# An mLSTM input stage without q and k: scores from one product with Wq Wk^T, gate weights folded through the blocks on VectorE

## The chip, the cores and the metric

The kernel runs on one core of one Trainium2 chip. It is written in a tile framework: the program says what is computed in which order, and the framework's scheduler places each engine's instructions and the semaphores between them. The metric is the device time of one execution in microseconds (us); the time before the change is the median of 3 runs, 1916.47 us (1914.49 to 1919.42).

The engines are PE (TensorE, matmuls; its weight loads are listed apart as PEld), DVE (VectorE), ACT (ScalarE), POOL (GpSimd) and SP (SyncE, which here only issues DMA transfers). Each engine works through its own instructions in order and waits on semaphores for the others.

## The reference, cut to what matters

Two layers of a decoder trunk over 256 tokens and 2048 features. The change is in the mLSTM group of layer 0. `xm` is a slice of the input projection, 256 tokens by 2048 channels; it is one of four slices of equal width (the other three belong to an RG-LRU group and to two gate paths). Each of Wq, Wk, Wv is block-diagonal, with 512 blocks of 4 by 4:

```
xmc = silu(causal_dwconv(xm, conv_w, conv_b))
q = block_diag(xmc, Wq);  k = block_diag(xmc, Wk);  v = block_diag(xm, Wv)
qkv = concat(q, k, v)                       # 256 x 6144
ig = qkv @ Wi + bi;  fg = qkv @ Wf + bf     # 8 heads each
# 8 heads of 256 channels, chunkwise; per head:
scores = (q @ k.T) / 16 * exp(decay matrix from ig, fg)
h = (scores @ v + ...) / normaliser
```

After that the kernel normalises each head, gates it, projects the concatenated groups with an output matrix and adds the residual. Layer 1 (RWKV-7) is not touched by the change.

## The kernel before

**The main stream on PE.** The weights of the four projections (input and output of both layers) are loaded in pieces of 256 by 512 (`load_w`, one 512 KB DMA from SP into one of four `raw` buffers). ACT rounds a piece to a high part `whi`, DVE forms the low part `wlo = raw - whi` (`split_w`, line 133 is the wrapper through which all ACT and DVE instructions pass), with three buffers each. `in_proj` goes through the eight pieces of 512 output columns; for a piece, `in_mms` issues 24 matmuls: the weights' high part times the high and the low part of the activations (16), then the low part times the high part (8). These have `gb` (two PSUM banks) as their output.

**The side work.** Everything else (convolutions, gates, recurrences) is written as generators with `yield`s that carry a time; `Weave` calls them between the matmuls of the main stream. PE's order is exactly the order in which the program issues matmuls (`InOrder`), so a side matmul whose operand is late holds up every main matmul behind it. DVE's and ACT's orders come from the scheduler; a piece's `whi` and `wlo` have high priority, and nothing that is emitted later goes ahead of them on their engines (`Behind`). Side results go to one of four `mb` PSUM banks.

**The mLSTM's input, `mlstm_in(c, xm)`.** The 2048 channels are done in four groups `c` of 512 (4 tiles of 128 channels, two heads). The projection of group `c` fills `gb`; ACT copies it to `xm`, and `mlstm_in(c)` runs as side work during the projection of the next group. Its generator's times are longer than that projection, so its last part, all of its matmuls, is issued in one run when `wv_.drain(prev)` empties it at the end of the next `in_proj`. This makes a **cluster** of side matmuls between the last main matmul of a projection and the first of the next. In order:

1. the convolution (ACT, then 3 DVE instructions `xc` a tile), `th` (ACT tanh) and `xm2 = 2 silu` (DVE);
2. `we`: 16 DVE products that spread the 4 by 4 blocks of Wq, Wk, Wv and Wv transposed into 128 by 128 block-diagonal tiles (`qkvs` holds the blocks, `blk` is the mask);
3. 8 matmuls of 256 columns for q and k (`mb<-xm,we` in the profile), copied out with a factor 0.5 by four ACT instructions to `qk`;
4. 8 matmuls of 128 columns for v (`mb<-we,xm`), copied to `vtok` by ACT;
5. 4 matmuls with 40 columns that take the v part of the gates' weights through Wv (`mb<-wif,we`), copied to `gv` by DVE;
6. 12 matmuls with 40 output rows for the gates: q and k against `wiff`, xm against `gv`; they alternate between two halves of the PE array's columns (output rows 0 to 39 and 64 to 103), and DVE adds the two halves to `gacc`;
7. the scores of two heads from `qk` (8 matmuls), copied to `S` by ACT with a factor 1/16.

`wiff` (the gates' weights, 128 by 48 by 40) is one 960 KB DMA in `tables()`, the generator that loads and prepares small tables during the first projection. The tile `wr` of the change takes the memory (tag `wg`) that `wiff` has here.

Of the kernel before, what the change touches and what calls it, by code (L numbers as in the profile page):

```python
# [144 lines left out]
def two_layers(ctx, tc, x, gpost, cst, selc, v0, v1, w_in0, w_out0, w_in1, w_out1, lruw, qkvw,  # L145
               wif, gbias, lora1, lora2, out):
    nc = tc.nc
    act, dve, pool, pe = nc.scalar, nc.vector, nc.gpsimd, nc.tensor
    PS = bass.MemoryType.PSUM
    wv_ = Weave(tc, 4)  # L150
    pe = wv_.pe = InOrder(tc, pe)
    dve, act = Behind(tc, dve), Behind(tc, act)
# [13 lines left out]
    def mbank():  # L166
        return pm.tile([P, 512], F32, name="mb", tag="mb")
# [252 lines left out]
    with ExitStack() as l0:  # L420
# [4 lines left out]
        def t4(name):  # L425
            return tp.tile([P, 4, T], F32, name=name, tag="t4")
# [27 lines left out]
        h = to_features(xs, [scale(ss[tt], s0) for tt in range(2)], lambda i: vs0("pre", i), (0, 0))  # L454


        wiff = c0.tile([P, 2048], F32, name="wif", tag="wg")[:, 0:1920].rearrange("p (a b) -> p a b", a=48)
        qkvs = c0.tile([P, 4, 16, 4], F32, name="qkvs")
# [4 lines left out]

        def tables():
            yield 2.1
            nc.sync.dma_start(qkvs, qkvw)
            nc.sync.dma_start(cs0, cst[:, NC1:NC])
            nc.sync.dma_start(sel, selc)
            nc.sync.dma_start(gbs, gbias)
# [12 lines left out]
            dve.tensor_scalar(s4, lt[:, 0, :], 4.0, None, MUL)  # L482
            dve.tensor_scalar(n4, lt[:, 0, :], -4.0, None, MUL)
            yield 7.7
            nc.sync.dma_start(wiff, wif)
            nc.sync.dma_start(vec1, v1)
            nc.sync.dma_start(cs[:, 128:NC1], cst[:, 128:NC1])
            act.copy(bonesr, cs0[:, 160:288])
# [10 lines left out]
        xm2s = []  # L499

        def mlstm_in(c, xm):
            xc = t4("xc")
            for f in range(4):
                i = 4 * c + f
# [7 lines left out]
            we = [t4("we") for _ in range(2)]  # L512
            wv = [w.rearrange("p a t -> p (a t)").rearrange("p (w f o) -> p w f o", w=2, f=4) for w in we]
            for m in range(4):
                for f in range(4):
                    dve.tensor_tensor(
                        wv[m // 2][:, m % 2, f, :].rearrange("p (b o) -> p b o", o=4),
                        qkvs[:, m, 4 * c + f, :].unsqueeze(1).broadcast_to([P, 32, 4]),
                        blk.unsqueeze(2).broadcast_to([P, 32, 4]), MUL)
                yield 4.0 if m == 3 else 1.0  # L520
            wq, wk, wvv, wvT = (wv[m // 2][:, m % 2] for m in range(4))
            qk = [t4("qk") for _ in range(2)]
# [6 lines left out]
            qt = lambda f: qk[f // 2][:, 2 * (f % 2), :]  # L529
            kt = lambda f: qk[f // 2][:, 2 * (f % 2) + 1, :]  # L530
            for tt in range(2):
                b = mbank()
                for f in range(4):
# [4 lines left out]
            gv = s0.tile([P, 160], F32, name="gv", tag="gv", bufs=1)  # L538
            b = mbank()
            for f in range(4):  # L540
                pe.matmul(b[:, f * 40:(f + 1) * 40], lhsT=wvT[:, f, :], rhs=wiff[:, 32 + 4 * c + f, :],
                          start=(f == 0), stop=True, skip_group_check=True)
            dve.tensor_copy(gv, b[:, 0:160])
            yield 0.96

            ops = []
            for f in range(4):
                i = 4 * c + f
                ops += [(wiff[:, i, :], qt(f)), (wiff[:, 16 + i, :], kt(f)), (gv[:, f * 40:(f + 1) * 40], xm[:, f, :])]
            b = mbank()  # L550
            for n, (w, r) in enumerate(ops):
                o = b[64 * (n % 2):64 * (n % 2) + 40, 0:T]
                pe.matmul(o, lhsT=w, rhs=r, start=(n < 2), stop=(n >= 10), skip_group_check=True)
                if n % 4 == 3:
                    yield 0.5
            for r in (slice(0, 40), slice(64, 104)):
# [5 lines left out]
            for hd in range(2):  # L562
                b = mbank()
                for j, (lo_, w_) in enumerate(((0, T), (P, P))):
                    o = b[:, 0:T] if j == 0 else b[:, T:T + P]
                    for f in range(2):
                        pe.matmul(o, lhsT=kt(2 * hd + f)[:, j * P:(j + 1) * P], rhs=qt(2 * hd + f)[:, lo_:T],
                                  start=(j == 0 and f == 0), stop=(f == 1), skip_group_check=True)
                activ(S[:, 2 * c + hd, :], b[:, 0:384], AF.Copy, scale=0.0625)
                yield 0.8  # L570

        gt = c0.tile([8, 8, T], F32, name="gt", tag="wg")
# [729 lines left out]
```

## Time and profile before

| what | value |
|---|---|
| median of 3 runs | 1916.47 us (1914.49 to 1919.42) |
| the profiled execution, its own time | 1918.1 us |
| its span, first to last instruction | 1916.3 us |
| mean granted TensorE clock | 0.995 |
| HBM read | 289.20 MB |
| the four clusters begin at | 64.35, 99.03, 133.83 and 168.63 us |

The profiled execution is one more run. Its own time is 1.8 us longer than its span, and 1.6 us over the median of the others. A row of a timeline gives the start, the length, the engine, the line, the operation, `out<-in` by the program's names (without buffer numbers), the shapes and the count; a bracket gives idle time ahead of it and what ended it. Lengths of consecutive instructions overlap a little, so the pace of an engine is read from the distance of two starts. A matmul of plain 32-bit floats shows as two records.

### The profile page before, as it was taken

The numbers are of one execution on the slowest core, as the hardware profiler recorded it, in microseconds if no ns is written. First come the engines' busy times: TensorE is split into PE (matmuls) and PEld (weight loads), VectorE is DVE, ScalarE is ACT, GpSimd is POOL, SyncE is SP. The second block draws the span as 40 slices with busy tenths as digits, with TensorE's granted clock in tenths as the row PEclk, the third lists the DMA queues.
The fourth block names the chain that finished last, engine by engine and source line by source line (L and its number), as shares of the span: only waits on it lengthen the run. The fifth ranks groups of instructions, "written<-read, shape, count | busy, mean of one in ns | idle before, by whom it ended". The sixth has DMA issues, their size and how long they took to land.

```text
span 1916.3 us, 39538 instructions
## 1 busy us (share of the span) xinstructions
PE 1890.5 (99%) x16506; PEld 1753.2 (91%) x16507; DVE 1394.7 (73%) x2302; ACT 1045.2 (55%) x1609; POOL 59.1 (3%) x84
## 2 busy tenths in 40 slices
PE   9999999999999999999999999999999999999998
PEld 8999999999888899989999999999999999997886
DVE  5667777767555679879689689597796896895544
ACT  6445666645444546555565555655655655555442
POOL 0000000000000000000000000000000000000000
PEclk9999999999999999999999999999999999999999
DMA  7333544445666444423434334344343433356654
GB/s 254 138 133 111 176 165 171 152 173 197 214 202 202 165 144 147 155 106 137 143 130 143 123 130 157 109 150 146 116 147 133 141 133 133 122 186 201 211 202 156
DMA packets 86947, 299.63 MB, mean 156 GB/s; under 512 B 9576, under 2 KB 12392, under 8 KB 86768
## 3 DMA queue, kind: packets, MB, share of 16 engines
q1 hardware_dynamic: 86768, 297.11, 45.0%
q8 instruction: 129, 2.11, 0.4%
q14 instruction: 50, 0.41, 0.1%
HBM read 289.20 MB, written 7.86 MB: 155 GB/s over the span
## 4 chain that ended last, share of the span: by engine, by line
PE 93%; DVE 4%; ACT 1%; issue 1%; DMA 1%; POOL 0%; SPq 0%; DVEq 0%; POOLq 0%; ACTq 0%
PE gb L117 75%; PE mb L117 17%; DVE wlo L133 2%; PE mb L120 1%; ACT whi L133 1%; DVE wb L133 1%; DMA raw<-in_w_in_dram 0%; DVE rt L133 0%; DVE Tb L133 0%; DMA xq<-in_x_dram 0%; DVE tf L133 0%; DVE Ab L133 0%; DVE yT L133 0%; ACT ZT L133 0%; ACT vt L133 0%
## 5 line engine op out<-in xcount | busy, mean ns | idle before, releaser
L133 DVE TENSOR_TENSOR wlo<-raw,whi 128x1024 fp32r<-128x1024 f32 x509 | 619.6, 1218 | 344.2 <-ACT whi L133 308.4
L133 ACT CAST whi<-raw 128x1024 fp32r<-128x1024 f32 x509 | 532.3, 1048 | 553.4 <-PE gb L117 505.1
L117 PE MATMUL gb<-hh,whi 128*128 128x256 f32 x3120 | 793.5, 290 | 2.9 <-ACT whi L133 2.9
L117 PE MATMUL gb<-hl,whi 128*128 128x256 f32 x3120 | 773.7, 284 | 0.5 <-DVE hl L133 0.5
L117 PEld LDWEIGHTS gb<-hh,whi 128*128 128x128 f32 x3120 | 598.8, 192 | 13.6 <-ACT whi L133 3.7
L117 PEld LDWEIGHTS gb<-hl,whi 128*128 128x128 f32 x3120 | 600.0, 192 | 1.9 <-DVE hl L133 1.1
L117 PE MATMUL gb<-hh,wlo 128*128 128x256 f32 x3120 | 454.0, 286 | 0.0
L117 PEld LDWEIGHTS gb<-hh,wlo 128*128 128x128 f32 x3120 | 405.5, 192 | 4.2 <-issue 0.7
L117 PE MATMUL gb<-whi,yl 128*128 128x512 f32 x500 | 136.9, 392 | 0.5 <-DVE yl L133 0.5
L117 PE MATMUL gb<-whi,yh 128*128 128x512 f32 x500 | 136.5, 392 | 0.0
L117 PE MATMUL gb<-wlo,yh 128*128 128x512 f32 x500 | 135.7, 390 | 0.0
L117 PEld LDWEIGHTS gb<-whi,yl 128*128 128x128 f32 x500 | 93.2, 188 | 20.4 <-DVE yl L133 0.9
L117 PEld LDWEIGHTS gb<-wlo,yh 128*128 128x128 f32 x500 | 93.5, 188 | 19.7
L117 PEld LDWEIGHTS gb<-whi,yh 128*128 128x128 f32 x500 | 93.0, 188 | 19.3
L133 DVE TENSOR_TENSOR Tb<-Tb,tf 64x31 f32<-64x31 f32 (+15 forms) x248 | 82.5, 333 | 6.1
L133 DVE TENSOR_TENSOR tf<-Ab,Tb 64x31 f32<-64x31 f32 (+15 forms) x248 | 81.8, 330 | 4.5
L117 PE MATMUL mb<-AR,BK 64*128 64x128 f32 (+1 forms) x1024 | 58.0, 253 | 7.0 <-DVE AR L133 6.0
L117 PEld LDWEIGHTS mb<-AR,BK 64*128 64x128 f32 (+1 forms) x1024 | 50.2, 161 | 13.3 <-PE gb L117 7.1
L133 DVE TENSOR_TENSOR UV<-mb,Gn 64x256 f32<-64x256 f32 x64 | 26.9, 421 | 34.6 <-PE mb L117 33.4
L133 ACT ACTIVATE zz<-kP,dv 128x256 f32<-128x256 f32 x64 | 32.3, 505 | 22.9 <-DVE kP L133 12.4
L117 PEld LDWEIGHTS mb<-UV,At 128*64 128x64 f32 (+1 forms) x1024 | 35.0, 137 | 10.3 <-issue 2.2
L1140 POOL TENSOR_TENSOR vr<-vr,mhalf 128x8 f32<-128x8 f32 x16 | 28.3, 1771 | 505.5 <-DVE vr L133 505.5
(259 smaller groups left out, 1859.7 us busy)
## 6 DMA issues: line engine op xcount, KB each, us to landing
raw<-in_w_in_dram SPq DMA_DIRECT2D x384, 512.0 KB, 3.2
raw<-in_w_out_dram SPq DMA_DIRECT2D x128, 512.0 KB, 4.2
y1d<-zt SPq DMA_DIRECT2D x7, 512.0 KB, 3.5
yraw<-y1d SPq DMA_DIRECT2D x7, 512.0 KB, 3.8
l<-in_lora_dram SPq DMA_DIRECT2D x8, 384.0 KB, 4.3
xq<-in_x_dram SPq DMA_DIRECT2D x8, 256.0 KB, 4.4
lw<-in_lruw_dram SPq DMA_DIRECT2D x4, 512.0 KB, 4.9
xr<-in_x_dram SPq DMA_DIRECT2D x8, 256.0 KB, 6.3
```

The costliest lines, as they stand in the source:

```text
L117: return self._chain(self.eng.matmul(*a, **k))
L120: return self._chain(self.eng.transpose(**k))
L133: r = op(*a, **k)
L1140: pool.tensor_tensor(vr, vr, mhalf[:, 0:8], ALU.pow)
```

## The change

- q and k are no longer formed. With X = Wq Wk^T (again 4 by 4 blocks), the scores are xmc X xmc^T. `tables()` loads the blocks of Wk four times over (`krep`, four DMAs), so that each partition holds all four rows of its block, and DVE forms the blocks of X in `Xc` by one product and one reduction. The cluster has 4 matmuls for `pp = X^T xm2` in place of the 8 for q and k, and the scores are taken from `pp` and `xm2`, with the factor 1/64.
- The gates' weights are multiplied by Wq, Wk and Wv beforehand, on DVE. Each `mlstm_in(c)` loads its part of them with each row repeated for the four rows of its block (`wr`, 24 DMAs of 40 KB), multiplies by the blocks (6 instructions `wr<-wr,qkvs`), reduces four ways (4 instructions, into `gw` and `gx`) and adds the two halves (2 instructions). The gates are then 8 matmuls, of `gw` against `xm2` and `xm`. The 4 matmuls and the copy for `gv` are gone, and so is the 960 KB DMA.
- Of the 16 products `we` a group, 8 are left (X and Wv).

The diff, cut to its core:

```diff
+        qkvs = c0.tile([P, 3, 16, 4], F32, name="qkvs")
+        krep = c0.tile([P, 4, 16, 4], F32, name="krep")
+        Xc = c0.tile([P, 4, 16], F32, name="Xc")
+        rows = lambda w: w.rearrange("(b o) r -> b o r", o=4)
...
-            nc.sync.dma_start(qkvs, qkvw)
+            nc.sync.dma_start(qkvs, qkvw[:, 0:3])
+            for i in range(4):
+                nc.sync.dma_start(krep[i:P:4].rearrange("p j t o -> p j (t o)"), rows(qkvw[:, 1].rearrange("p t o -> p (t o)")))
...
-            nc.sync.dma_start(wiff, wif)
+
+            dve.tensor_tensor(krep, krep, qkvs[:, 0].unsqueeze(1).broadcast_to([P, 4, 16, 4]), MUL)
+            dve.tensor_reduce(Xc, krep, mybir.AxisListType.X, ADD)
+            dve.tensor_scalar(qkvs[:, 0:2], qkvs[:, 0:2], 0.5, None, MUL)
...
         def mlstm_in(c, xm):
+            wr = c0.tile([P, 2, 3, 2, 160], F32, name="wr", tag="wg")
+            for o2 in range(2):
+                for m in range(3):
+                    src = rows(wif[:, 16 * m + 4 * c:16 * m + 4 * c + 4].rearrange("p t n -> p (t n)"))[:, 2 * o2:2 * o2 + 2]
+                    for i in range(4):
+                        nc.sync.dma_start(wr[i:P:4, o2, m], src)
...
-            for m in range(4):
+            for m in range(2):
...
-                yield 4.0 if m == 3 else 1.0
+                yield 1.0
+            wx, wvv = we[:, 0], we[:, 1]
+
+            gw = s0.tile([P, 2, 160], F32, name="gw", tag="gw", bufs=1)
+            gx = s0.tile([P, 160], F32, name="gx", tag="gx", bufs=1)
+            for o2 in range(2):
+                for m in range(3):
+                    w = qkvs[:, m, 4 * c:4 * c + 4, 2 * o2:2 * o2 + 2].rearrange("p t o -> p o t")
+                    r = wr[:, o2, m].rearrange("p o (t n) -> p o t n", t=4)
+                    dve.tensor_tensor(r, r, w.unsqueeze(3).broadcast_to([P, 2, 4, 40]), MUL)
+                for to, ms in ((0, slice(0, 2)), (1, slice(2, 3))):
+                    d = gx if o2 else gw[:, to]
+                    dve.tensor_reduce(d, wr[:, o2, ms].rearrange("p m o n -> p n (m o)"), mybir.AxisListType.X, ADD)
+                    if o2:
+                        dve.tensor_tensor(gw[:, to], gw[:, to], gx, ADD)
+                    yield 1.5
+            pp = t4("pp")
+            for f2 in range(2):
                 b = mbank()
-                pe.matmul(b[:, 0:T], lhsT=wq[:, f, :], rhs=xm2[:, f, :], start=True, stop=True, skip_group_check=True)
-                pe.matmul(b[:, T:2 * T], lhsT=wk[:, f, :], rhs=xm2[:, f, :], start=False, stop=True, skip_group_check=True)
-                activ(qk[f // 2][:, 2 * (f % 2):2 * (f % 2) + 2, :], b.rearrange("p (a t) -> p a t", a=2), AF.Copy, scale=0.5)
+                for f in range(2):
+                    pe.matmul(b[:, f * T:(f + 1) * T], lhsT=wx[:, 2 * f2 + f, :], rhs=xm2[:, 2 * f2 + f, :],
+                              start=(f == 0), stop=True, skip_group_check=True)
+                act.copy(pp[:, 2 * f2:2 * f2 + 2, :], b.rearrange("p (a t) -> p a t", a=2))
                 yield 0.6
...
-            for f in range(4):
-                pe.matmul(b[:, f * 40:(f + 1) * 40], lhsT=wvT[:, f, :], rhs=wiff[:, 32 + 4 * c + f, :],
-                          start=(f == 0), stop=True, skip_group_check=True)
-            dve.tensor_copy(gv, b[:, 0:160])
-            yield 0.96
...
-                ops += [(wiff[:, i, :], qt(f)), (wiff[:, 16 + i, :], kt(f)), (gv[:, f * 40:(f + 1) * 40], xm[:, f, :])]
+                ops += [(gw[:, 0, f * 40:(f + 1) * 40], xm2[:, f, :]), (gw[:, 1, f * 40:(f + 1) * 40], xm[:, f, :])]
...
-                        pe.matmul(o, lhsT=kt(2 * hd + f)[:, j * P:(j + 1) * P], rhs=qt(2 * hd + f)[:, lo_:T],
+                        pe.matmul(o, lhsT=xm2[:, 2 * hd + f, j * P:(j + 1) * P], rhs=pp[:, 2 * hd + f, lo_:T],
```

On PE nothing else moves: outside the four clusters its order is the same. Two places show what the scheduler makes of the rest.

DVE around the second cluster (group `c = 1`), before. `wlo` is the main stream's low part; the first `wlo` here belongs to the last but one piece that can be prepared ahead of the cluster, the second waits until PE is done with the last piece ahead of the cluster; `xc` is already the convolution of the next group:

```order
L133 TENSOR_TENSOR wlo<-raw,whi 128x1024
L133 TENSOR_TENSOR we<-qkvs,cs_112 128x128 x9
L133 TENSOR_TENSOR wlo<-raw,whi 128x1024
L133 TENSOR_TENSOR we<-qkvs,cs_112 128x128 x3
L133 SCALAR_TENSOR_TENSOR xc<-xm,vec_97,xc 128x255
L133 COPY gv<-mb 128x160
L133 SCALAR_TENSOR_TENSOR xc<-xm,vec_97,xc 128x254
L133 SCALAR_TENSOR_TENSOR xc<-xm,vec_97,xc 128x255
L133 SCALAR_TENSOR_TENSOR xc<-xm,vec_97,xc 128x253
L133 SCALAR_TENSOR_TENSOR xc<-xm,vec_97,xc 128x254
L133 SCALAR_TENSOR_TENSOR xc<-xm,vec_97,xc 128x253
L133 TENSOR_TENSOR gacc<-gacc,mb 40x256 x2
```

The same place after the change, from the `wr` product that follows the last `we` (five `we` stand between the first `wlo` and this row) to the last sum `gw`, which the gates' matmuls need:

```order
L133 TENSOR_TENSOR wr<-wr,qkvs 128x320
L133 TENSOR_REDUCE gw<-wr 128x160
L133 TENSOR_TENSOR wlo<-raw,whi 128x1024
L133 TENSOR_REDUCE gw<-wr 128x160
L133 TENSOR_TENSOR wr<-wr,qkvs 128x320 x3
L133 TENSOR_REDUCE gx<-wr 128x160
L133 SCALAR_TENSOR_TENSOR xc<-xm,vec_97,xc 128x255
L133 TENSOR_TENSOR gw<-gw,gx 128x160
L133 SCALAR_TENSOR_TENSOR xc<-xm,vec_97,xc 128x254
L133 TENSOR_REDUCE gx<-wr 128x160
L133 SCALAR_TENSOR_TENSOR xc<-xm,vec_97,xc 128x253
L133 TENSOR_TENSOR gw<-gw,gx 128x160
```

Two of the six products stand earlier, among the previous `xc`. Four products, all the reductions and both sums stand here, behind `wlo` and between the next group's `xc`. The other three clusters have the same order (in the fourth, `yc` of the RG-LRU's convolution stands where `xc` does).

SP from the first projection to the second group, before (`raw` are the main stream's pieces, the first piece is ahead of these rows):

```order
L218 DMA raw<-in_w_in_dram 128x1024 x4
L485 DMA wif<-in_wif_dram 128x1920
L486 DMA vec_81<-in_v_dram 128x384
L487 DMA cs<-in_cst_dram 128x386
L218 DMA raw<-in_w_in_dram 128x1024 x34
```

and after:

```order
L218 DMA raw<-in_w_in_dram 128x1024 x4
L493 DMA vec_81<-in_v_dram 128x384
L494 DMA cs<-in_cst_dram 128x386
L218 DMA raw<-in_w_in_dram 128x1024 x4
L514 DMA wr<-in_wif_dram 32x2x160 x24
L218 DMA raw<-in_w_in_dram 128x1024 x14
L514 DMA wr<-in_wif_dram 32x2x160 x24
L218 DMA raw<-in_w_in_dram 128x1024 x8
```

Four times 24 small DMAs now stand between the pieces. Each DMA takes one of eight completion semaphores in turn and waits until the DMA that had it before has landed; from the second batch on the first of the 24 also waits until DVE has read the last `wr`.

More of the change, by code (lines that the diff above doesn't have):

```diff
@@ L454, in two_layers @@
         h = to_features(xs, [scale(ss[tt], s0) for tt in range(2)], lambda i: vs0("pre", i), (0, 0))
-        wiff = c0.tile([P, 2048], F32, name="wif", tag="wg")[:, 0:1920].rearrange("p (a b) -> p a b", a=48)
-        qkvs = c0.tile([P, 4, 16, 4], F32, name="qkvs")
+        qkvs = c0.tile([P, 3, 16, 4], F32, name="qkvs")
+        krep = c0.tile([P, 4, 16, 4], F32, name="krep")
+        Xc = c0.tile([P, 4, 16], F32, name="Xc")
+        rows = lambda w: w.rearrange("(b o) r -> b o r", o=4)
         sel = c0.tile([8, 8, P], F32, name="sel")
@@ L511, in mlstm_in @@
             dve.scalar_tensor_tensor(xm2, th, 1.0, xc, ADD, MUL)
-            we = [t4("we") for _ in range(2)]
-            wv = [w.rearrange("p a t -> p (a t)").rearrange("p (w f o) -> p w f o", w=2, f=4) for w in we]
-            for m in range(4):
+            we = t4("we").rearrange("p a t -> p (a t)").rearrange("p (w f o) -> p w f o", w=2, f=4)
+            for m in range(2):
                 for f in range(4):
+                    i = 4 * c + f
                     dve.tensor_tensor(
-                        wv[m // 2][:, m % 2, f, :].rearrange("p (b o) -> p b o", o=4),
-                        qkvs[:, m, 4 * c + f, :].unsqueeze(1).broadcast_to([P, 32, 4]),
+                        we[:, m, f, :].rearrange("p (b o) -> p b o", o=4),
+                        (Xc[:, :, i] if m == 0 else qkvs[:, 2, i, :]).unsqueeze(1).broadcast_to([P, 32, 4]),
@@ L519, in mlstm_in @@
                         blk.unsqueeze(2).broadcast_to([P, 32, 4]), MUL)
-                yield 4.0 if m == 3 else 1.0
-            wq, wk, wvv, wvT = (wv[m // 2][:, m % 2] for m in range(4))
-            qk = [t4("qk") for _ in range(2)]
-            for f in range(4):
+                yield 1.0
[13 more added lines that the diff above has]
+                    yield 1.5
@@ L528, in mlstm_in @@
                 yield 0.6
-            qt = lambda f: qk[f // 2][:, 2 * (f % 2), :]
-            kt = lambda f: qk[f // 2][:, 2 * (f % 2) + 1, :]
             for tt in range(2):
@@ L537, in mlstm_in @@
                 yield 0.78
-            gv = s0.tile([P, 160], F32, name="gv", tag="gv", bufs=1)
-            b = mbank()
-            for f in range(4):
-                pe.matmul(b[:, f * 40:(f + 1) * 40], lhsT=wvT[:, f, :], rhs=wiff[:, 32 + 4 * c + f, :],
-                          start=(f == 0), stop=True, skip_group_check=True)
-            dve.tensor_copy(gv, b[:, 0:160])
-            yield 0.96
             ops = []
             for f in range(4):
-                i = 4 * c + f
-                ops += [(wiff[:, i, :], qt(f)), (wiff[:, 16 + i, :], kt(f)), (gv[:, f * 40:(f + 1) * 40], xm[:, f, :])]
+                ops += [(gw[:, 0, f * 40:(f + 1) * 40], xm2[:, f, :]), (gw[:, 1, f * 40:(f + 1) * 40], xm[:, f, :])]
             b = mbank()
@@ L552, in mlstm_in @@
                 o = b[64 * (n % 2):64 * (n % 2) + 40, 0:T]
-                pe.matmul(o, lhsT=w, rhs=r, start=(n < 2), stop=(n >= 10), skip_group_check=True)
+                pe.matmul(o, lhsT=w, rhs=r, start=(n < 2), stop=(n >= 6), skip_group_check=True)
                 if n % 4 == 3:
@@ L566, in mlstm_in @@
                     for f in range(2):
-                        pe.matmul(o, lhsT=kt(2 * hd + f)[:, j * P:(j + 1) * P], rhs=qt(2 * hd + f)[:, lo_:T],
+                        pe.matmul(o, lhsT=xm2[:, 2 * hd + f, j * P:(j + 1) * P], rhs=pp[:, 2 * hd + f, lo_:T],
                                   start=(j == 0 and f == 0), stop=(f == 1), skip_group_check=True)
-                activ(S[:, 2 * c + hd, :], b[:, 0:384], AF.Copy, scale=0.0625)
+                activ(S[:, 2 * c + hd, :], b[:, 0:384], AF.Copy, scale=0.015625)
                 yield 0.8
```

## Prediction

> **What bounds the kernel now.** I read the page first, then the chain that ended last, then the stretch that the change touches.
>
> ```profile
> span 1916.3 us, 39538 instructions
> PE 1890.5 (99%) x16506; PEld 1753.2 (91%) x16507; DVE 1394.7 (73%) x2302; ACT 1045.2 (55%) x1609; POOL 59.1 (3%) x84
> PE 93%; DVE 4%; ACT 1%; issue 1%; DMA 1%; POOL 0%; SPq 0%; DVEq 0%; POOLq 0%; ACTq 0%
> ```
>
> PE is never without work for long and makes up 93% of the chain. So PE work that goes away shortens the time, as long as PE does not wait in its place. The second cluster, as PE ran it:
>
> ```profile
> 99.03 3.62 PE L117 MATMUL mb<-xm,we 128*128 128x256 f32 x16
> 102.48 1.95 PE L117 MATMUL mb<-we,xm 128*128 128x128 f32 x16
> 104.27 0.98 PE L117 MATMUL mb<-wif,we 128*128 128x40 f32 x8
> 105.18 0.63 PE L117 MATMUL mb<-qk,wif 128*40 128x256 f32 x4
> ...
> 108.07 2.88 PE L117 MATMUL mb<-qk 128*128 128x256 f32 x16
> 110.71 0.36 PE L117 MATMUL gb<-hh,whi 128*128 128x256 f32 x1
> ```
>
> From start to start: 3.45 us for q and k, 1.79 for v, 0.91 for `gv`, 2.89 for the twelve gate matmuls, 2.64 for the scores, 11.68 in all, no bracket with idle time. DVE and ACT meanwhile:
>
> ```profile
> 96.47 1.23 DVE L133 TENSOR_TENSOR wlo<-raw,whi 128x1024 fp32r<-128x1024 f32 x1
> 97.62 1.90 DVE L133 TENSOR_TENSOR we<-qkvs,cs 128x128 f32<-128x128 f32 x9
> 99.44 1.22 DVE L133 TENSOR_TENSOR wlo<-raw,whi 128x1024 fp32r<-128x1024 f32 x1
> 100.57 0.69 DVE L133 TENSOR_TENSOR we<-qkvs,cs 128x128 f32<-128x128 f32 x3
> 104.89 0.48 DVE L133 SCALAR_TENSOR_TENSOR xc<-xm,vec,xc 128x255 f32<-128x255 f32 x1 [3.63 <-ACT xc L133]
> 105.40 0.32 DVE L133 COPY gv<-mb 128x160 f32<-128x160 f32 x1
> 105.64 2.17 DVE L133 SCALAR_TENSOR_TENSOR xc<-xm,vec,xc 128x254 f32<-128x254 f32 x5
> ```
>
> DVE has its `we` ready when PE begins (99.03) and then idles 3.63 us. It sits off the path, with room; but the change puts its new work just here.
>
> **What goes from PE.** Of q and k half, 3.45 / 2 = 1.73 us; all of `gv`, 0.91; of the gates 4 of 12, 2.89 / 3 = 0.96. That is 3.60 us a cluster, 14.4 us in four. The scores and v stay as they are.
>
> **What PE must now wait for.** After the change PE is done with `pp` and v at 99.03 + 1.73 + 1.79 = 102.55 and comes to the gates, the second of which needs the last sum into `gw`. When is it ready? I go through DVE's new order with these rows:
>
> ```profile
> L133 DVE TENSOR_TENSOR we<-qkvs,cs 128x128 f32<-128x128 f32 x64 | 14.2, 285 | 0.0
> L133 DVE TENSOR_TENSOR Dt<-Dt,S 128x384 f32<-128x384 f32 x8 | 4.4, 554 | 2.1 <-ACT Dt L133 2.0
> L133 DVE TENSOR_REDUCE vr<-yT 128x8 f32<-128x512 f32 x8 | 5.5, 687 | 2.6 <-ACT yT L133 2.4
> ```
>
> Products of 128 and 384 elements take 285 and 554 ns: 1.05 ns an element over about 150 ns. A reduction of 512 elements, 687 ns, lies on the same line, so I price reductions by their input. Nine `we` follow each other at (99.44 - 97.62) / 9 = 0.20 us, some 0.08 less than one lasts, so I take 0.08 off each for the overlap: 0.40 us for a `wr` product or a reduction of 320, 0.74 for one of 640, 0.24 for a sum of 160; 0.42 for an `xc` (five in 2.17) and 1.13 for `wlo` (99.44 to 100.57).
>
> - Five `we` and one product from 97.62: 99.03. The first reduction (640): 99.77.
> - `wlo`, free to run since 99.44 as before, now runs from 99.77 to 100.90.
> - Reduction (320) 101.30; three products 102.51; about 0.1 for the wait on the last of them; reduction (640) 103.35.
> - `xc`, sum, `xc`, reduction (320), `xc`: 0.42 + 0.24 + 0.42 + 0.40 + 0.42 = 1.90, to 105.25. ACT has the input of `xc` ready: its two copies of `xm` and its convolution stand behind two copies `pp` where four `qk` stood.
> - The last sum ends 0.32 later, 105.57, and about 0.1 for the semaphore: PE goes on at 105.67.
>
> So PE waits from 102.55 to 105.67, 3.1 us, but for one gate matmul of 0.24 between the two sums. Seven more gates at 0.24: 107.36, where 108.07 was. **Of the 3.60 us a cluster, 0.7 are left: 2.8 us in four.** Queued behind the waiting gate are the scores and the whole next projection, since PE's order is fixed.
>
> **What the wait does to the clock.** In layer 1 the trace has stretches in which PE's clock is at half. Two of them, each behind the 3.41 us ahead of it (a row gives the busy time of PE, PEld, DVE, ACT and POOL, then the granted clock):
>
> ```profile
> 824.25:827.66 3.41, 2.59 (x30) 2.30 (x31) 3.24 (x10) 0.51 (x1) 0.00 (x0) 1.00 0.44 156
> 827.66:831.08 3.42, 3.42 (x19) 3.42 (x18) 1.50 (x4) 1.55 (x3) 0.00 (x0) 0.50 0.00 0
> 1059.77:1063.18 3.41, 3.11 (x73) 2.86 (x72) 3.35 (x7) 3.34 (x7) 0.00 (x0) 1.00 0.65 251
> 1063.18:1066.60 3.42, 3.42 (x19) 3.42 (x18) 0.41 (x1) 1.27 (x2) 0.00 (x0) 0.50 0.47 161
> ```
>
> And PE's instructions at full clock, at half clock, and in the third of these stretches:
>
> ```profile
> 821.86 0.28 PE L117 MATMUL gb<-hh,whi 128*128 128x256 f32 x1
> 821.98 0.28 PE L117 MATMUL gb<-hl,whi 128*128 128x256 f32 x1
> ...
> 828.09 0.41 PE L117 MATMUL gb<-hh,whi 128*128 128x256 f32 x1
> 828.30 0.41 PE L117 MATMUL gb<-hl,whi 128*128 128x256 f32 x1
> ...
> 1060.44 2.21 PE L117 MATMUL mb<-TT,ZT 32*32 32x32 f32 x64 [0.30 <-ACT ZT L133]
> ```
>
> Ahead of a half-clock stretch PE was busy for 2.59 and 3.11 us of 3.41, but 2.21 us of the latter were matmuls on a 32 by 32 corner: what counts is work of the whole array, and 1.2 us of it (3.41 - 2.21) did not hold the clock. A 3.41 us stretch that takes in the 3.1 us wait holds far less; one that catches only part of it still has gates on 40 of 128 columns beside it. I estimate that in 9 of 10 positions the clock falls. The price: main matmuls 0.21 us apart instead of 0.12, so 3.42 x (1 - 0.12 / 0.21) = 1.5 us at most, about 1.2 as part of the slow stretch falls into the wait itself. Four clusters: 4 x 0.9 x 1.2 = 4.3 us. Before, the clock stays full in the clusters:
>
> ```profile
> 99.03:110.80 11.77, 11.77 (x83) 9.52 (x82) 5.93 (x16) 5.98 (x12) 0.00 (x0) 1.00 0.22 82
> ```
>
> The Trainium skill, "TensorE: Matmul & The Clock Gate", section "What's actually happening", says that the clock falls to half after at least one idle window of about 3.4 us. The row 1059.77:1063.18, busy for 3.11 us, contradicts that reading. By it the wait, broken by one gate, would cost no clock; the rival "the clock stays" below is worked out from rows alone.
>
> **DVE's reads.** The reductions read elements 640 bytes apart. The trace has products on 31 elements 128 bytes apart (747.21, first step of the recursion) and on 31 adjacent ones (798.57, last step):
>
> ```profile
> 747.21 0.20 DVE L133 TENSOR_TENSOR Tb<-Tb,tf 64x31 f32<-64x31 f32 x1
> 798.57 0.18 DVE L133 TENSOR_TENSOR Tb<-Tb,tf 64x31 f32<-64x31 f32 x1
> ```
>
> 0.02 us over 31 elements is 0 to 0.65 ns each. The late reductions have 640 + 320 + 640 + 320 = 1920 elements: 0 to 1.2 us a cluster, 0 to 5 us in all. A gain is excluded, as nothing makes a reduction shorter than its pace here. I take 0.1 us a cluster, near the lower end, since the difference may be a constant. The Trainium skill, "SBUF — State Buffer", section "Specifications (TRN2)", says that SBUF has 16-byte lines and that each step to another line costs something; it gives no price, and the two rows allow little of it.
>
> **SP and the start.** SP's rows:
>
> ```profile
> 0.73 1.82 SPq L437 DMA_DIRECT2D xq<-in_x_dram  x4
> 66.00 0.33 SPq L218 DMA_DIRECT2D raw<-in_w_in_dram  x1
> 80.44 0.33 SPq L218 DMA_DIRECT2D raw<-in_w_in_dram  x1
> raw<-in_w_in_dram SPq DMA_DIRECT2D x384, 512.0 KB, 3.2
> ```
>
> Issues follow at 1.82 / 4, some 0.47 us, so 24 take 11 us. From the second batch on they stand in a gap of SP of 14.4 us, between two pieces (66.00 and 80.44). They may start when the previous `wr` is read, at the last reduction (about 70), and end near 82: the next piece comes 2 us late and lands 3.2 later, while PE needs it 24 matmuls of 0.12, 2.9 us, ahead of the cluster at 99.03. Hidden. The first batch stands among the pieces at the end of the first projection and holds the next one up by at most its 11 us, which four buffers of 2.9 us each about cover; with `krep`'s four DMAs ahead of the second piece, and without the 960 KB, I take 0.3 us for both (0 to 2). Fewer ACT copies and fewer `we` are off the path: nothing.
>
> **Sum** against the profiled execution: 1918.1 - 2.8 + 4.3 + 0.4 + 0.3 = 1920.3, so +2.2. The median of the runs is 1.6 lower; on it the change gives 1918.7, and I predict 1919.
>
> **Rivals.**
> - *The clock stays* (or falls in few clusters): -2.8 + 0.7 = -2.1, 1914.4 on the median. For it: the threshold is read from two places. Against: the two pairs of rows above. Chance 0.17.
> - *The sums are ready in time*, and PE keeps the full 14.4: 1902. Against: `wlo` cannot start before 99.44, and with it 5.8 us of DVE work stand ahead of the last sum's end, while PE arrives at 102.55. Chance 0.05.
> - *Slower, by the reductions*: 160 short groups or distant reads at twice the pace add 1.05 x 1920 = 2.0 us a cluster to the wait, 8 us, and another 1 us of clock: 1928. It decides (over 0.3%, 5.7 us) from 0.5 ns an element. For it: no row has short groups. Against: the rows of reductions and of distant elements. Chance 0.2.
> - *Slower, by SP*: with 1 us an issue, first batch and gap overflow; 24 us instead of 11 put the pieces, by my estimate, some 9 us too late once and 2.5 us three times, 1935. Against: no issue lasts over 0.47. Chance 0.05.
>
> **How the numbers follow.** My forecast has 0.53. About 0.3% is what a measurement of this kernel tells from no change. Faster: the second rival and a tail of the first, 0.07. Slower: the third but for its small end, SP, a tail of the forecast, 0.26. Same: 0.67. The range leaves out the full gain, SP and the upper end of the reductions: 1912.5 to 1927.
>
> **What would show it.** PE idle of about 3 us in each cluster, ended by DVE `gw`; the gates starting 6.6 us after the cluster's begin; a half-clock stretch after most clusters; reductions of 0.82 us (640) and 0.49 (320); `raw` landing before ACT wants it. A cluster without that idle time, or waits on `raw`, would make the prediction wrong.

## The result and the profile after

The changed kernel takes 1930.95 us (median of 4 runs, 1927.7 to 1932.02), the kernel before 1916.22 (1914.49 to 1919.42): ratio 1.0072, 95% interval 1.0054 to 1.009. It is slower by some 14 us, where "the same, 1919" was forecast. The profiled execution took 1927.7 us. One execution of the run with sums in place of reductions was in a slower state (2261.03 us, granted clock 0.747) and is not in that run's median.

Page of the changed kernel (span, busy time by engine, shares of the chain), then PE's longest entry in the list of waits (us in total, times, longest):

```profile
span 1925.9 us, 39475 instructions
PE 1883.1 (98%) x16410; PEld 1742.0 (90%) x16411; DVE 1411.4 (73%) x2317; ACT 1040.6 (54%) x1601; POOL 59.0 (3%) x84
PE 89%; DVE 6%; ACT 1%; issue 1%; SPq 1%; DMA 1%; POOL 0%; DVEq 0%; POOLq 0%; ACTq 0%
PE mb L117 <- DVE gw L133: 14.7, 8, 3.3
```

PE works 7.4 us less than before (1890.5 - 1883.1), yet the span is 9.6 longer: DVE has come into the chain, and PE waits for `gw` eight times, twice a cluster. Where the loss has arisen shows the chain, in which the same long piece of the output projection of layer 0 begins at 468.35 before (first row) and at 480.36 after (second):

```profile
468.35 174.61 PE gb L117 x768
```

```profile
480.36 174.59 PE gb L117 x768
```

In these two executions 12.0 us stand by the end of layer 0. (2.4 of it do not show at the end: layer 1 of the changed kernel happened to have 3 half-clock stretches in it and not 5, besides one at the very end of both.) The medians lie further apart, 14.7 us; the profiled execution is the fastest of the four. The second cluster of the changed kernel on PE; brackets are the idle time ahead of a row:

```profile
103.65 1.89 PE L117 MATMUL mb<-xm,we 128*128 128x256 f32 x8
105.38 1.95 PE L117 MATMUL mb<-we,xm 128*128 128x128 f32 x16
110.14 0.60 PE L117 MATMUL mb<-xm,gw 128*40 128x256 f32 x2 [2.82 <-DVE gw L133]
111.47 3.53 PE L117 MATMUL mb<-xm,gw 128*40 128x256 f32 x14 [0.73 <-DVE gw L133]
114.93 2.92 PE L117 MATMUL mb<-pp,xm 128*128 128x256 f32 x16
```

The cluster begins at T = 103.65. PE is through with v at T + 3.52, as forecast, and passes the second gate at 111.47 = T + 7.82, where T + 6.64 was forecast. The gates behind it take 3.46 us in place of some 1.7: the clock. The stretch that holds the wait, and the one behind it (busy PE, PEld, DVE, ACT, POOL, then the granted clock):

```profile
108.20:111.60 3.40, 0.73 (x4) 0.28 (x6) 3.40 (x9) 0.52 (x2) 0.00 (x0) 1.00 0.30 120
111.60:115.00 3.40, 3.40 (x15) 1.30 (x13) 1.17 (x3) 0.00 (x0) 0.00 (x0) 0.50 0.21 57
```

All four clusters have such a half-clock stretch; PE was busy for 0.60 to 1.26 us of the 3.40 ahead of it. DVE ahead of the gates, in the same cluster:

```profile
103.81 0.48 DVE L133 TENSOR_TENSOR wr<-wr,qkvs 128x320 f32<-128x320 f32 x1
104.21 1.27 DVE L133 TENSOR_REDUCE gw<-wr 128x160 f32<-128x640 f32 x1
105.40 1.21 DVE L133 TENSOR_TENSOR wlo<-raw,whi 128x1024 fp32r<-128x1024 f32 x1
106.53 0.48 DVE L133 TENSOR_REDUCE gw<-wr 128x160 f32<-128x320 f32 x1
...
108.14 1.23 DVE L133 TENSOR_REDUCE gx<-wr 128x160 f32<-128x640 f32 x1
```

The products and the reductions of 320 last what was forecast (0.48); the reductions of 640 last 1.25, not 0.82. And the first product starts at T + 0.16 where the forecast had it end at T. SP and the first pass: the first 24 issues, what ACT then waits for, and PE:

```profile
25.75 16.13 SPq L514 DMA_DIRECT2D wr<-in_wif_dram  x24
41.98 1.95 SPq L218 DMA_DIRECT2D raw<-in_w_in_dram  x4
```

```profile
45.50 1.04 ACT L133 CAST whi<-raw 128x1024 fp32r<-128x1024 f32 x1 [2.23 <-DMA raw<-in_w_in_dram]
46.59 0.39 PE L117 MATMUL gb<-hh,whi 128*128 128x256 f32 x1 [1.58 <-ACT whi L133]
```

An issue takes 16.13 / 24 = 0.67 us, not 0.47; the next piece of `raw` is late, and PE waits, which the four buffers were to prevent. How late the first cluster then begins varies: at 66.85 us here (64.35 before), at 66.35 to 71.37 in the traces of the five experiments below that keep the 24 issues on SP. Where PE's wait at this place is 2.6 us or more (three of the six traces) a half-clock stretch follows, where it is 1.6 to 1.9 us (the other three) none does.

### The profile page after: what moved, and what is told of

It is laid out like the page before. It is cut to its first block, busy times and chain, and to the rows that moved or that the text cites. A ratio compares the mean times of both kernels' runs of the same rounds, so it can differ in the third digit from the quotient of the medians.

```text
span 1925.9 us, 39475 instructions
## 1 busy us (share of the span) xinstructions
PE 1883.1 (98%) x16410; PEld 1742.0 (90%) x16411; DVE 1411.4 (73%) x2317; ACT 1040.6 (54%) x1601; POOL 59.0 (3%) x84
## 4 chain that ended last, share of the span: by engine, by line
PE 89%; DVE 6%; ACT 1%; issue 1%; SPq 1%; DMA 1%; POOL 0%; DVEq 0%; POOLq 0%; ACTq 0%
PE gb L117 72%; PE mb L117 15%; DVE wlo L133 2%; PE mb L120 1%; SPq L514 1%; ACT whi L133 1%; DVE wb L133 1%; DMA raw<-in_w_in_dram 1%; DVE wr L133 0%; DVE gx L133 0%; DVE gw L133 0%; DVE rt L133 0%; DVE we L133 0%; DVE Tb L133 0%; DVE hl L133 0%
## 5 line engine op out<-in xcount | busy, mean ns | idle before, releaser
L133 DVE TENSOR_TENSOR wlo<-raw,whi 128x1024 fp32r<-128x1024 f32 x509 | 619.6, 1218 | 340.1 <-ACT whi L133 307.0
L133 ACT CAST whi<-raw 128x1024 fp32r<-128x1024 f32 x509 | 532.3, 1048 | 549.1 <-PE gb L117 492.5
L133 DVE TENSOR_TENSOR Tb<-Tb,tf 64x31 f32<-64x31 f32 (+15 forms) x248 | 82.6, 333 | 6.1
L133 DVE TENSOR_TENSOR tf<-Ab,Tb 64x31 f32<-64x31 f32 (+15 forms) x248 | 81.9, 330 | 4.5
L133 DVE TENSOR_TENSOR UV<-mb,Gn 64x256 f32<-64x256 f32 x64 | 26.9, 421 | 34.2 <-PE mb L117 33.1
L133 ACT ACTIVATE zz<-kP,dv 128x256 f32<-128x256 f32 x64 | 32.3, 505 | 22.9 <-DVE kP L133 12.4
L117 PE MATMUL mb<-UV,At 128*64 128x64 f32 (+1 forms) x1024 | 43.8, 228 | 0.0
```

Source lines behind the costliest of these rows:

```text
L117: return self._chain(self.eng.matmul(*a, **k))
L133: r = op(*a, **k)
```

## The experiments

The theory to begin with: a late start of 2.5 us, and 2.1 to 2.3 us from one cluster to the next, because the wait for `gw` and the half clock behind it eat more than the removed work. Rivals: the small transfers are the main loss; or VectorE as a whole is late. Each ratio below is to the kernel before, run beside the experiment (medians 1915.37 to 1917.10 us), so times of different experiments are best compared by their ratios.

**Gates behind the scores.**

```diff
-            ops = [] ... 8 gate matmuls (16 records), gacc
             for hd in range(2):
                 ... 8 score matmuls (16 records)
+            ops = [] ... 8 gate matmuls (16 records), gacc
```

> The change with one edit: in each cluster the 16 gate matmuls are issued behind the 16 of the scores instead of ahead of them. Theory (the changed kernel loses 12.0 us by the end of layer 0: about 2.5 at the start behind the longer DMA issue, and 4 x 2.3 in the clusters, where PE waits 2.8 + 0.7 us for gw and then runs 3.4 us at half clock): the scores last 2.6 us at full clock and fill most of the wait; what is left is about 0.3 + 0.7 us a cluster. That alone is 4 x 2.5 = 10 us; where the half-clock stretch goes too, 4 x 1.6 more. Time 1914 to 1921, same or slightly faster than before. Rival A (the transfers and their issue are the main loss, the wait only shows it): less than 3 us gained, 1928 or more. Rival B (VectorE as a whole is too late, so that PE then waits for wlo in the next products instead): about half, 1925, with a row of waits for wlo.

Measured: 1928.32 us, ratio 1.0067 (1.0055 to 1.0079). The theory missed by over 7 us. The time is rival A's. VectorE is late, as rival B had it, but PE waits for `xm`, `we` and `gw`, not for `wlo`. Part of the loss lies at the start: in this execution the first cluster began at 69.50 us, 2.65 later than in the changed kernel, behind a longer wait for `raw`. Cluster 1 waited 0.24 + 0.73 us for `gw`, at full clock; the third cluster shows what happens to the others, on PE, then on ACT and DVE:

```profile
141.22 1.53 PE L117 MATMUL mb<-xm,we 128*128 128x256 f32 x6 [1.95 <-DVE xm L133]
...
150.12 0.60 PE L117 MATMUL mb<-xm,gw 128*40 128x256 f32 x2 [1.92 <-DVE gw L133]
```

```profile
134.22 1.05 ACT L133 CAST whi<-raw 128x1024 fp32r<-128x1024 f32 x1 [6.35 <-DMA raw<-in_w_in_dram]
```

```profile
135.31 1.23 DVE L133 TENSOR_TENSOR wlo<-raw,whi 128x1024 fp32r<-128x1024 f32 x1 [6.17 <-ACT whi L133]
```

DVE stands 6.17 us at a `wlo` whose `raw` is late, with the convolution, `xm` and the fold queued behind it. SP says why `raw` is late: 24 issues begin when the last reduction has read the previous `wr`, and `raw` goes on only behind them:

```profile
113.47 16.36 SPq L514 DMA_DIRECT2D wr<-in_wif_dram  x24
129.92 13.20 SPq L218 DMA_DIRECT2D raw<-in_w_in_dram  x7
```

So there is a ring: last sum of `gw`, 16 us of SP, `raw`, `whi`, `wlo`, convolution, `xm`, next `gw` (the run with one DMA and gates last, below, tests it). Its length is near 37 us (the first gates stand at 76.03, 112.79, 150.12, 187.26), and in the changed kernel this bound lies hidden just behind the wait for `gw`.

**One DMA in place of 24.** The host lays `wif` and Wk out with the rows repeated (no arithmetic):

```diff
-            for o2 in range(2): for m in range(3): for i in range(4):
-                        nc.sync.dma_start(wr[i:P:4, o2, m], src)
+            nc.sync.dma_start(wr.rearrange("p a m o r -> p (a m o r)"), wif[:, c, :])
-            for i in range(4):
-                nc.sync.dma_start(krep[i:P:4]..., ...)
+            nc.sync.dma_start(krep, qkvw[:, 4:8])
```

> The change with one edit: wr and krep come from arrays laid out in the order of the tiles (rows repeated four times), so that one DMA a cluster stands in place of 24 and one in place of 4; the bytes that land are the same. Theory: only the start is lost to the issue (first product piece 0.6 us late, the one at 46.6 us 1.6 us late, 2.5 in all); the clusters keep their wait and their half clock. Time 1928 to 1929, the wait for gw stays 14 to 15 us. Rival A (the issue on SP and the transfers are the main loss): 8 us or more gained, 1923 or less. Rival B (the bytes, not the issue, delay raw): no gain, 1930.5 to 1931.5.

Measured: 1927.3 us, 1.0058 (1.0046 to 1.007): 3.6 less than the changed kernel's 1930.95, a little more than the theory. The intervals of the two ratios overlap, but the end of layer 0 also comes 3.8 us earlier in the trace (476.58, not 480.36). The wait for `gw` stays (13.9 us). By itself SP costs the start (the first cluster begins at 64.15, not 66.85) and little else; the third cluster had two half-clock stretches this time and the fourth none.

**Sums in place of reductions.**

```diff
-                    dve.tensor_reduce(d, wr[:, o2, ms].rearrange("p m o n -> p n (m o)"), X, ADD)
+                    if to == 0:
+                        dve.tensor_tensor(wr[:, o2, 0], wr[:, o2, 0], wr[:, o2, 1], ADD)
+                    dve.tensor_tensor(d, wr[:, o2, 2 * to, 0], wr[:, o2, 2 * to, 1], ADD)
```

> The change with one edit: each of the four strided reductions of a cluster is replaced by sums of two contiguous rows (for the pair of 640: one sum of 320 and one of 160; for that of 320: one of 160). Theory (the reductions of 640 at 1.25 us are what made the wait longer than forecast): VectorE's path to the last gw gets shorter by 2 x (1.19 - 0.40 - 0.24) + 2 x (0.40 - 0.24) = 1.4 us a cluster, PE's wait by the same, 5.6 us in all: 1925. If the shorter wait also saves some of the half-clock stretches, 1.6 us for each of them more: down to 1919. Rival (the place in VectorE's queue behind wlo and xc sets the wait, not the pace of the reductions): under 2 us, 1929 or more.

Measured: 1925.22 us, 1.0052 (1.0036 to 1.0067), the forecast; but the trace is split. Clusters 1 and 3 wait 1.7 + 0.6 us, as computed, at full clock; the fourth, like the second, waits longer than with the reductions:

```profile
147.63 0.60 PE L117 MATMUL mb<-xm,gw 128*40 128x256 f32 x2 [1.72 <-DVE gw L133]
...
183.96 0.60 PE L117 MATMUL mb<-xm,gw 128*40 128x256 f32 x2 [3.80 <-DVE gw L133]
```

The second and fourth run into half clock as well. Ahead of them ACT waits 3.4 and 3.6 us for `raw`. A cluster that is quick is paid for in the next one: the ring again.

**PE kept busy in the wait.** Ten matmuls of the tile of ones ahead of the gates (their result is overwritten):

```diff
             b = mbank()
+            keep_warm(10, b)
             for n, (w, r) in enumerate(ops):
```

> The change with one edit: ten matmuls of the bf16 tile of ones (no use, written over at once) ahead of the gate matmuls in each cluster, so that PE works while it waits for gw. Theory (the idle stretch itself brings the half clock, 3.4 us in each cluster, worth about 1.6): the first gate matmul stays where it is or comes up to 0.5 us later, the half-clock stretch behind it goes: 4 x 1.1 to 1.6 = 4.4 to 6.4 us, 1924.5 to 1926.5. Rival A (the half clock comes whatever PE does in the wait): 0 to 4 x 1 us slower, since the ten run at half speed as well, 1931 to 1935. Rival B (the half clock in the clusters is paid back in layer 1, where the changed kernel had 3 such stretches and before 5): 1929 or more, with 5 in layer 1 again.

Measured: 1930.49 us, 1.0081 (1.0068 to 1.0094): the forecast missed. Clusters 1 and 3 have 0.6 us of the first wait left and no half clock; 2 and 4, with `raw` late, have 2.1 and 2.0 left and 6.8 us at half clock each. The time is rival B's, but not its cause: layer 1 has 3 half-clock stretches, as in the changed kernel, not 5. So these three edits were tried again together with the one DMA, which takes the ring away.

**One DMA and sums.**

> Two edits to the change: wr and krep by one DMA each (as in the run with one DMA, 1927.3 us) and contiguous sums in place of the reductions. Theory now (two things bound a cluster: VectorE's path to gw, and behind it the 24 issues of wr on SP, which hold back the pieces of raw of the next pass; whatever makes a cluster faster with the 24 issues in place meets late raw, then late wlo, then late conv, xm and gw): with the issues gone, each of the four waits for gw is 1.7 + 0.6 us as in clusters 1 and 3 of the run with the sums alone, not 3.3 to 4.1 as in its clusters 2 and 4. 4 x 1.25 = 5 us less than with one DMA alone, 1922; without the half-clock stretches, up to 4 x 1.6 less again, 1916. Rival (the coupling has another cause, such as PE's own pace against VectorE's queue): clusters 2 and 4 still wait over 3 us, 1924 to 1926.

Measured: 1916.45 us, 1.0003 (0.9995 to 1.0012): the time of the kernel before, at the theory's lower end. The first three clusters wait 1.7 + 0.57, the fourth 2.1 + 0.56, all at full clock; the third:

```profile
134.05 1.95 PE L117 MATMUL mb<-we,xm 128*128 128x128 f32 x16
137.72 0.60 PE L117 MATMUL mb<-xm,gw 128*40 128x256 f32 x2 [1.72 <-DVE gw L133]
138.89 1.92 PE L117 MATMUL mb<-xm,gw 128*40 128x256 f32 x14 [0.57 <-DVE gw L133]
140.74 2.88 PE L117 MATMUL mb<-pp,xm 128*128 128x256 f32 x16
```

With 2.3 us of waiting left a cluster, the change just breaks even.

**One DMA and PE kept busy.**

> Two edits to the change: one DMA each, and ten matmuls of ones in the wait ahead of the gates. Theory: wait and pace of VectorE stay, PE is busy in the wait; in the run with the ten matmuls and the 24 issues, clusters 1 and 3 (0.6 us of the first wait left) showed no half clock and clusters 2 and 4 (2.1 left, late raw) showed 6.8 us of it each. With one DMA all four are like 1 and 3: no half clock in the clusters; against the run with one DMA (13.7 us at half clock in three clusters) about 6 to 7 us less: 1920.5 to 1922. Rival (the half clock comes from something else than the idle stretch, or is made up by VectorE's pace: PE at full clock only waits longer at the next place): 1926 or more.

Measured: 1920.35 us, 1.002 (1.0011 to 1.003), 7 us under one DMA alone and just below the forecast. PE waits no less than in the changed kernel (2.32 us of ones and 0.59, then 0.80):

```profile
103.79 2.32 PE L117 MATMUL mb<-ones 128*128 128x512 bf16 x10
106.70 0.63 PE L117 MATMUL mb<-xm,gw 128*40 128x256 f32 x2 [0.59 <-DVE gw L133]
108.12 1.92 PE L117 MATMUL mb<-xm,gw 128*40 128x256 f32 x14 [0.80 <-DVE gw L133]
```

but the gates run in 1.92, not 3.53, and the clusters follow each other in 35.4 us, where the changed kernel's take 37.1 (103.65 to 140.71). The difference, 1.6, is the price of one half-clock stretch.

**One DMA and gates last.**

> Two edits to the change: one DMA each, and the gate matmuls behind the scores. Theory: the run with the gates last alone (1928.3) lost its gain to raw, which came late behind the 24 issues (ScalarE waited 6 us for it, VectorE's queue stood behind wlo, and PE then waited 1.4 to 2.0 us for xm and 1.9 for gw in clusters 2 and 3); cluster 1, with raw in time, waited 0.24 + 0.73 and ran at full clock. With one DMA all four are like cluster 1: 31.1 + 1.0 us a cluster against 34.7 before, 4 x 2.6 = 10 us under before: 1905 to 1908; where a half-clock stretch comes here and there, up to 1912. Rival (VectorE's queue is late by itself, as the xm wait shows, whatever SP does): waits for xm stay in clusters 2 to 4, 1920 or more.

Measured: 1909.79 us, 0.9962 (0.9949 to 0.9975), faster than before. Each cluster waits 0.23 to 0.35 and 0.73 us, at full clock, none waits for `xm`. That is the theory's mechanism, but the time is above its 1905 to 1908: the clusters follow each other in 32.84 us, not the 32.1 counted on. The same edit was worth 2.6 us with 24 issues (1930.95 to 1928.32, with ratios that overlap, so nothing clear of noise) and is worth 17.5 without (1927.3 to 1909.79).

**One DMA, sums, fold early.** The block of products and sums stands ahead of the third of the four convolutions:

```diff
             for f in range(4):
                 i = 4 * c + f
+                if f == 2:
+                    ... products and sums of gw, gx (yield 1.0 each)
                 conv(xc[:, f, :], ...)
...
-            gw = ... products and reductions behind the we block
```

> Three edits to the change: one DMA each, contiguous sums, and the products and sums of gw issued ahead of the third of the four convolutions, some 15 us before PE needs gw, instead of behind them. Theory: PE waits for nothing in the clusters: 3.6 us a cluster less than before, 14.4 in all, plus 0.5 at the start: 1901 to 1903. Rival A (VectorE's work, moved ahead, makes wlo or xm late, since it does as much as ever): waits for xm or we of 1 us or more in each cluster and, with them, half-clock stretches: 1908 to 1915. Rival B (the clock drops in the clusters also without a wait): 1907 or so.

Measured: 1907.91 us, 0.9957 (0.9945 to 0.9969): rival A's waits, but milder than it had them. PE waits for `gw` nowhere, but in each cluster 0.6 to 1.0 us for `xm` and `we`, with no half-clock stretch in the clusters; the one in layer 0 stands at the start (11.2 us), behind a wait of 2.6 us for `dg`.

**One DMA, sums, gates last.**

> Three edits to the change: one DMA each, contiguous sums, and the gate matmuls behind the scores. Theory: the scores (2.6 us) cover the wait of 1.7 that the sums leave, and most of the second; in the clusters 0 to 0.4 us of waiting is left where the run with one DMA and the gates last had 0.24 + 0.73, and neither xm nor we is late, as they were where the fold was moved ahead: 0.6 to 0.97 us a cluster less than 1909.8, 2.4 to 3.9 in all, 1906 to 1907.5, about 10 us under the kernel before. Rival (what is left of the gap between 1909.8 and the 1901 that the removed matmuls promise does not lie in these waits): no gain, 1909 to 1911.

Measured: 1904.8 us, 0.9933 (0.992 to 0.9945), below the forecast. In the first three clusters PE waits for nothing; the second:

```profile
95.87 1.89 PE L117 MATMUL mb<-xm,we 128*128 128x256 f32 x8
97.60 1.95 PE L117 MATMUL mb<-we,xm 128*128 128x128 f32 x16
99.38 2.78 PE L117 MATMUL mb<-pp,xm 128*128 128x256 f32 x16
102.10 2.25 PE L117 MATMUL mb<-xm,gw 128*40 128x256 f32 x16
104.28 0.39 PE L117 MATMUL gb<-hh,whi 128*128 128x256 f32 x1
...
455.94 174.59 PE gb L117 x768
```

The last row is the marker of layer 0's end: 12.4 us earlier than before (468.35), 3.1 of the 3.6 us a cluster that were forecast to go. The cluster shown takes 8.41 us (95.87 to 104.28), 3.27 less than the 11.68 before: the eight gates take 2.18 us to the next main matmul, where 8 x 0.24 = 1.93 was counted, and the scores 2.72, not 2.64. The fourth takes 8.79, with a pause of about a quarter of a microsecond ahead of its third gate.

**Fold early with 24 issues.** As the run with the fold early, without the one DMA:

> The change with contiguous sums and the fold ahead of the third convolution, but with its 24 issues of wr and 4 of krep in place: against the run with the fold early and one DMA (1907.9) only the issues differ. Theory (the 24 issues cost time at the start, and in the later clusters only through a ring: last sum of gw, release of wr, 16 us of issue, raw, wlo, conv, next gw): with the fold early, wr comes free some 15 us sooner, the ring is no longer the longest way, and what is left is the start, 2.5 to 3.5 us: 1910 to 1912. Rival A (16 us of SP in each pass hold back raw wherever they start): late raw or late wr in each pass, 1.5 to 3 us each, 1915 to 1922. Rival B (the issues cost nothing when nobody waits for gw): 1908.

Measured: 1913.38 us, 0.9981 (0.9971 to 0.9991), between theory and rival A. At the start `raw` is late, more than in the changed kernel (ACT waits 3.3 us for it, where it waited 2.2, and PE runs into half clock behind it); in the clusters PE waits 2.7 us in all for `xm`, 1.7 at most at once, 1.0 for `we`, and never for `gw`. The mechanism is the theory's, the start was priced too low: the first cluster begins 5.5 us later than with one DMA (71.37, not 65.88), and the next three then follow as fast (in 96.6 us, against 97.6), though ACT waits 2.1 and 3.0 us for `raw` ahead of the last two.

**The issues alone, in the kernel before.**

```diff
         def mlstm_in(c, xm):
+            wr = c0.tile([P, 2, 3, 2, 40], F32, name="wr", tag="wr")
+            ... 24 DMAs into wr[i:P:4, o2, m], 40 columns each
```

> The kernel before with one thing added: the 24 issues of wr at the start of each cluster, in the form of the change but with 40 columns in place of 160 (a quarter of the bytes, for room), into a tile that nothing reads, so that they wait for no earlier reader. Theory (as such the issues delay only the first pass, where the next piece of raw came 1.6 us late; later passes run from pieces loaded ahead): 1.5 to 2.5 us slower than before, ratio 1.001. Rival (SP's 16 us delay raw in each pass, whoever reads wr): 4 to 8 us slower, ratio 1.002 to 1.004.

Measured: 1924.56 us, 1.0036 (1.0022 to 1.0051), 7.5 us over the 1917.10 beside it: above the theory, at the rival's figure, though the third and fourth passes lose nothing. The first cluster starts 2.0 us late (66.35, not 64.35), and the second another 3.9: with no fold to wait for, SP issues the second batch as early as 52.4, and this time the late `raw` meets the cluster itself. ACT and PE there:

```profile
72.62 1.04 ACT L133 CAST whi<-raw 128x1024 fp32r<-128x1024 f32 x1 [2.41 <-DMA raw<-in_w_in_dram]
73.57 0.59 ACT L133 ACTIVATE qk<-mb 128x512 f32<-128x512 f32 x1
```

```profile
74.21 0.63 PE L117 MATMUL mb<-qk,wif 128*40 128x256 f32 x4 [1.65 <-ACT qk L133]
```

The copy of `qk` stands behind a cast that waits for `raw`, PE waits for `qk`, and the clock falls from 75.3 to 78.7. Clusters 3 and 4 then follow in 34.8 us, as before. So the issues cost without the fold too, in the first two passes; that the later ones are spared because pieces lie ready is the theory's reading, and no run separates it.

**The 24 transfers from GpSimd's queue**, with sums and gates last, and the host's layout as it was:

```diff
-                        nc.sync.dma_start(wr[i:P:4, o2, m], src)
+                        on_pool(wr[i:P:4, o2, m], src)
...
+    def on_pool(o, i):
+        r = pool.dma_start(o, i)
+        ... ordered behind the two rs of the start
```

> The change with contiguous sums and the gate matmuls last, and with its 24 small transfers of wr a cluster and 4 of krep in place, but issued from GpSimd's queue (behind its two rs of the start) and not from SP's. Nothing else differs from the run with one DMA, sums and gates last (1904.8) but the number of transfers, and from the changed kernel's own form but the queue. Theory (SP's queue is what costs: raw stands behind 16 us of issue): raw is never late, the wait for gw stays under 0.5 us a cluster, 1904 to 1908. Rival A (96 small transfers slow raw whatever the queue): a late raw of 1.5 to 2 us in the first pass and 1.5 us or more in each later one, 1911 or more. Rival B (GpSimd issues too slowly, so that wr itself is late and VectorE's queue stands behind its products): PE waits over 1 us for gw or xm in each cluster, 1912 or more.

Measured: 1905.92 us, 0.9942 (0.9928 to 0.9955): the theory. The transfers are as many and take 12.9 us a batch to issue (the first 15.5); `raw` does not stand behind them:

```profile
102.08 12.90 POOL L326 DMA_DIRECT2D wr<-in_wif_dram  x24 [18.66 <-DVE gx L133]
...
455.96 174.59 PE gb L117 x768
```

The first cluster begins at 64.38 us, where it began at 66.35 to 71.37 in all six traces with the 24 issues on SP. So it was SP's queue, not the number of transfers. (The same two edits with the 24 issues left on SP were not run.)

## Why the prediction was wrong, point by point

Measured at the end of layer 0, by the terms of the sum:

| term | forecast | measured |
|---|---|---|
| work gone from PE | -14.4 | -13.8 |
| wait for the second gate, less the one gate in it | 4 x 2.9 | 3 x 4.06 + 4.5 = 16.7 |
| half clock | 4.3 | about 6.2 |
| distant reads | 0.4 | in the wait |
| SP, start | 0.3 | 2.5 |
| sum | +2.2 | +12.0 (terms: 11.6) |

- *What goes from PE* nearly held: v ends at T + 3.52, as forecast, but the seven gates behind the wait take 1.85 us at full clock (138.89 to 140.74 in the run with one DMA and sums), not 7 x 0.24 = 1.69: 0.16 us a cluster. *Wait, clock, SP*: each mechanism was the forecast one, in its place; each was priced too low, so that all these errors lie on one side.
- **The wait, failed step: "I price reductions by their input".** The two reductions of 640 take 1.17 us of DVE each (104.21 to 105.40, 108.14 to 109.29), not 0.74: 0.86 us a cluster. Taken away in the run with one DMA and sums, they shortened the wait from 2.82 + 0.73 to 1.72 + 0.57. This is the third rival's mechanism ("decides from 0.5 ns an element"), given 0.2; at (1250 - 150) / 640 = 1.72 ns an element it is 0.67 over pace, but for the reductions of 640 alone: (480 - 150) / 320 = 1.03. Of the two causes that the rival named, the short groups are not it. The changed kernel has one reduction of groups of four that lie side by side, and it costs (410 - 150) / 256 = 1.02 ns an element:

  ```profile
  28.41 0.41 DVE L133 TENSOR_REDUCE Xc<-krep 128x64 f32<-128x256 f32 x1
  ```

  What is left is the distance, with four rows 640 bytes apart in a group and not with two; this is read from the three forms, no run changes the distance alone. The row by which I priced distant reads (31 elements, 0.02 us) had one hop pattern and did not show it. The Trainium skill, "Vector Engine (DVE) Microarchitecture Reference", section "5.2 Measured stream behaviour on trn2 (trn3 not measured)", gives 1.73 ns a column where one source hops 4 KiB at every element, and the full rate where a single read stream alternates between two regions 16 KiB apart. The rows here agree in number, with hops of 640 bytes: 1.72 for four regions, 1.03 for two. The page of the Trainium skill cited in the prediction (16-byte lines, no price) does not tell the two apart.
- A second part of the wait: DVE began 0.56 us later than forecast (first product ended at T + 0.56, not T). The two `wr` products that the order puts ahead, among the `xc` (96.87 and 97.66, 0.4 us each), were not priced, and DVE has no gap from 95.33 on to take them; that they are the cause is read from these rows, no run takes them away alone. The rest of DVE's path came out 0.24 us shorter than forecast: 0.56 + 0.86 - 0.24 is the 1.18 by which the second gate was late.
- **The clock, failed step: "1.5 us at most, about 1.2", in 9 of 10.** It fell in all four clusters, at 1.3 to 1.6 us each (length of a cluster against the same with ones in the wait, 12.3 us in the first three; in the last, the longer wait taken off). The bound came from the main matmuls, 0.12 to 0.21 us a step; gates in f32 go from 0.22 to 0.42. By the Trainium skill, "TensorE: Matmul & The Clock Gate", section "What's actually happening", with its idle window as the prediction read it, no cluster would have dropped; one did behind a stretch with 0.73 us of work in 3.40.
- **SP, failed step: "which four buffers of 2.9 us each about cover".** 24 issues took 16.1 us, not 11, because the issue of a small transfer takes 0.67 us here and not the 0.47 of the large ones. In this trace the first pass lost 1.6 us at 46.59, and `krep` 0.6 at 19.06 (that wait is there in all five traces with `krep`'s four issues on SP, and in none of the others).
- *"Hidden"* for the later batches was right for clusters 2 and 3 of the changed kernel; ahead of the fourth ACT waited 2.2 us for `raw`, and the wait for `gw` was 3.3 instead of 2.8. As a statement on the bound it was wrong: it held because PE was waiting anyway.
- *The rival "sums ready in time, 1902"* comes near what the edit is worth: with hardly anything late, 1904.8.

**What stays open:** what within a 3.4 us stretch decides on the clock: with waits of 1.92 + 0.73 us in both, it fell in the third cluster of the gates-last run and not in the second. Open too is how much of the 14.7 us between the medians lies at the start, which varies from one execution to the next.

## What to carry to other kernels

When work moves from a full engine to one with room, ask when that one can be done, and put what needs it last: here the order of two blocks, the queue of 24 small transfers and the shape of a sum turned +14 us into -11. Two bounds of nearly the same length hide each other: an edit against one then shows nothing clear of noise (2.6 us) and with the other gone as well shows all (17.5), so try fixes in pairs before a theory is dropped. A transfer's issue is a cost to the queue in which it stands, and its price falls on whatever is next there.

## What the runs showed of the hardware

- A reduction over groups of four elements 640 bytes apart: 1.72 ns an element above some 150 ns, over groups of two: 1.03, over groups of four adjacent elements: 1.02; the sums of 320 and 160 contiguous elements that replace it: 0.48 and 0.31 us.
- The issue of a transfer of 32 rows in two pieces of 640 bytes takes 0.67 us on SP and 0.54 on GpSimd (12.9 / 24); a transfer of 960 KB 0.33 (0.43 the first).
- Ten bf16 matmuls of 128 x 512 in a wait (2.32 us) kept the clock at full with 0.59 + 0.80 us of idle time around them.
